# Other places in TensorE's queue for the ends of the mixer's branches and for x's transposes, in a two-layer hybrid encoder

## The chip, the cores and the metric

The kernel runs on one core of a Trainium2 chip. The metric is the device time of one execution in microseconds (us); the time before is the median of three runs. Names used throughout: PE is TensorE (matmuls and transposes), ACT is ScalarE, DVE is VectorE, POOL is GpSimd, SP is SyncE, which starts the weight loads. PSUM is the memory that matmuls write to. Every engine works through its own queue in order; an instruction at the head of a queue that waits for another engine holds up all that stands behind it.

## The reference

The input x is 256 tokens by 1024 features, float32; there are two layers. In each:

```python
xn = rms_norm(x, norm_mix_g[l]);  h = xn @ w_in[l]      # all branches and 4 merge gates from one product
ya = conv_module(glu, ...)        # GLU, depthwise conv of width 31, LayerNorm over channels, silu
yb = gla_branch(gq, gk, gv, gr, glr, ...)   # chunked gated linear attention, then RMS over each head, * silu(gr)
yc = window_attention(q, k, v, sink)        # softmax(q k) v, 4 heads
yd = pool_branch(pin, ...)                  # mean pooling of widths 2 to 16, minus self, per-group map
proj   = einsum('btnc,ncd->btnd', stack([ya, yb, yc, yd]), w_branch)   # each branch, 256 -> 1024
merged = sum(sigmoid(gate) * proj, axis=2)
x = x + merged @ w_out
x = x + square(relu(rms_norm(x, norm_ffn_g) @ w_up)) @ w_down           # 1024 -> 4096 -> 1024
```

and a final RMSNorm.

## The kernel before

**Matrix products.** Each float32 product is done as three matmuls on operands split into a high and a low part: hi·hi, lo·hi and hi·lo. In mm3 (L303 to L305) the weights are stationary and 256 tokens stream; in mm3t (L312 to L314) the activations are stationary and 512 columns of weights stream. So L303, L304, L305 and L312, L313, L314 are nearly all of PE's work, and a row's "mm<-hi,ysh" says whose: xh/xl are the normalised x of the mixer, ysh/ysl the split output of a branch, mh/ml the merged branches, fh/fl the input of the MLP, hh/hl its hidden values.

**Weights** come in pieces of 128 x 1024 values. SP loads a piece into a raw buffer, ACT casts it to hi (L276), DVE subtracts to get lo (L277). The pieces form one list in order of use and are split four ahead of PE. Raw has three buffers, hi and lo five each.

**Order.** The code is written as a program order with priorities; a scheduler turns it into one queue for each engine. Work inside `urgent()` gets a priority 4000 higher, so that it goes ahead of what was written earlier and is ready at the same time. `tc.issue_after(ins)` puts work behind the instruction `ins` on its engine. PSUM tiles come from two pools of four buffers: mm (mmt) for the large products, ax (axt) for the rest, the transposes among them.

**A layer's mixer.** After the input products, attention and GLA are generators; the string TURNS hands out six turns to attention and twelve to GLA. Then `conv_branch` writes the whole convolution branch. The gates and the branches' projections follow in the order of GATE_SEQ: gate A (pooling), gate B (attention) and so on, each in two halves of 512 columns, with the projection ("br") of a branch some steps behind its gate:

```python
GATE_SEQ = (("gate", A, 0), ("gate", A, 1),
    ("gate", B, 0), ("br", A, 0), ("gate", B, 1), ("br", A, 1),
    ("gate", C, 0), ("br", B, 0), ("gate", C, 1), ("br", B, 1),
    ("gate", L, 0), ("br", C, 0), ("gate", L, 1),
    ("br", L, 0), ("br", C, 1), ("br", L, 1))     # B attention, C GLA, L convolution
```

A gate is 48 matmuls, a projection 12. The scheduler mixes the branches' small instructions into the gates' matmuls. The ends of the branches are these chains:

- Attention: transposes of its result (L654 on PE), then split_y: ACT casts to ysh (L447), DVE subtracts to ysl (L448).
- GLA: the product with the state (L853 on PE), squares (L864 and L865 on ACT), the load of ACT's table for Ln and Exp (L866), sums over a head (L871 and L872 on PE), a reciprocal square root (L332 and L333 on ACT, then L335 to L337 on DVE), a product (L876 on DVE), split_y.
- Convolution: taps on DVE and ACT; a sum over channels for the mean (L524 on PE), L525 on DVE, a square on ACT (L527) with a table load (L528) behind it, the sum for the variance (L532 on PE), the reciprocal square root, a Tanh with its table load (L540), split_y.

**Around the MLP.** The out projection accumulates in ax; DVE adds it to x in two halves of 512 columns (L1087). turn_x then transposes x back (L431 on PE, 128 x 128 blocks, eight a half), and split_x makes fh (L420, ACT) and fl (L421, DVE) of it. The same turn_x makes xh and xl for the next layer, after DVE has added the MLP's result to x (L1150).

Of the kernel before, what the change touches and what calls it, by code (L numbers as in the profile page):

```python
# [171 lines left out]
def trunk_kernel(ctx: ExitStack, tc: tile.TileContext, x, w, prm, wup, poolw, cst, out, depth, dbg=None):  # L172
# [125 lines left out]
    def mm3(o, wt, k, c0, xs, kx, start, stop):  # L298
        wh, wl = wt
        xh, xl = xs  # L300
        a = wh[:, k, c0 : c0 + P]
        b = wl[:, k, c0 : c0 + P]
        mm(o, a, xh[:, kx, :], start=start, stop=False, skip_group_check=True)  # L303
        mm(o, a, xl[:, kx, :], start=False, stop=False, skip_group_check=True)  # L304
        mm(o, b, xh[:, kx, :], start=False, stop=stop, skip_group_check=True)  # L305

# [187 lines left out]

    def conv_branch(l):
# [48 lines left out]

# [4 lines left out]
    def attention_branch(l, qkv, y):  # L549
# [76 lines left out]
        for it in range(2):  # L626
            for jt in range(2):
                tp = axt((P, 4, P))
                for h in range(4):
                    nc.tensor.transpose(tp[:, h, :], ps_[it][:, h % 2, h // 2, jt * P : (jt + 1) * P], ident)  # L630
                S.copy(pt[:, jt, :, it * P : (it + 1) * P], tp)

            ot = axt((P, 4, 64))
            for h in range(4):
                g = h // 2
                for jt in range(2):
                    mm(  # L637
                        ot[:, h, :],
                        pt[:, jt, h, it * P : (it + 1) * P],
                        qkv[:, jt, 384 + 64 * g : 448 + 64 * g],  # L640
                        start=jt == 0,
                        stop=jt == 1,
                    )
            V.tensor_tensor(
                on[:, it].rearrange("p (g r) e -> p g r e", g=2),
                ot.rearrange("p (g r) e -> p g r e", g=2),
                dens[it].rearrange("p r g -> p g r").unsqueeze(3).broadcast_to([P, 2, 2, 64]),
                ALU.mult,
            )
            yield  # L650
        o = axt()
        for it in range(2):
            for g in range(2):
                nc.tensor.transpose(  # L654
                    o[:, g, it * P : (it + 1) * P], on[:, it, 2 * g : 2 * g + 2].rearrange("p h e -> p (h e)"), ident
                )
        y[BR_ATT] = split_y(o)

# [17 lines left out]

    def gla_gates(l, glr, wup_t):
        gt = axt((P, 2, P))
# [11 lines left out]
        z = axt()  # L690
        for d in range(2):
            mm(z[:, d, :], wur[:, d, :], glt, start=True, stop=True)
        zb = g2()
# [16 lines left out]
    def gla_branch(l, px, qk, v, gy, ys):  # L710
# [150 lines left out]
        with urgent():  # L861
# [5 lines left out]
            V.tensor_tensor(sl, sq, sh.bitcast(F32), ALU.subtract)  # L867
            V.tensor_tensor(gy, gy, o, ALU.mult)
            ss = axt()
            for t in range(2):  # L870
# [23 lines left out]
    for l in range(depth):  # L894
# [32 lines left out]
        def gvl(i, k0, k1):  # L927
            wt = piece(l, ("gvl", i))
            for k in range(k1 - k0):
                for it in range(2):  # L930
                    mm3t(gps[it], xs, k0 + k, it, wt, k, k0 + k == 0, k0 + k == 7)

        def part256(ps, key, i):
            wt = piece(l, (key, i))
            for k in range(4):
                for t in range(2):
                    kk = 4 * i + k
                    mm3(ps[:, t, :], wt, k, t * P, xs, kk, kk == 0 and t == 0, kk == 7)

        cuts = list(enumerate(GVL_CUTS[l == 0]))  # L940
        for i, (k0, k1) in cuts if l == 0 else cuts[:2]:
            gvl(i, k0, k1)
        ps_g, ps_a = mmt(), None
# [13 lines left out]
        for it in range(2):  # L957
            gla_in(l, gps[it], it, v, glr, R)
        px = gla_gates(l, glr, wup_t)

        for i in range(2) if l == 0 else (1,):
# [3 lines left out]
        for i in range(2) if l == 0 else (1,):  # L965
            part256(ps_a, "glu0", i)
        conv_in(ps_a, ps_g, R)
# [42 lines left out]

        def gate(n, h):
            pss = [mmt((P, 512)) for _ in range(2)]
            for i in range(4):
                wt = piece(l, (("gate", n, h), i))
                for k in range(2):
                    for it in range(2):
                        kk = 2 * i + k
                        mm3t(pss[it], xs, kk, it, wt, k, kk == 0, kk == 7)
            for it in range(2):
# [22 lines left out]
        def turn_merged(h):  # L1042
            for f in (2 * h, 2 * h + 1):
                with urgent():
# [36 lines left out]
        for h in range(2):  # L1081
            for i in (2, 3):
                out_part(i, h)
# [16 lines left out]
        def up(c, parts=(0, 1)):  # L1100
# [3 lines left out]
            for i in parts:  # L1104
                wt = piece(l, (("up", c), i))
                for k in range(4):
                    for t in range(2):
                        kk = 4 * i + k
                        mm3(ps[:, t, :], wt, k, t * P, fx, kk, kk == 0 and t == 0, kk == 7)
            if 1 not in parts:  # L1110
                return
            r = gh_p.tile([P, 2, T], F32, tag="gh", name=nm("r"))
# [21 lines left out]
        for i in range(2):  # L1134
            for c in range(2):
                up(c, (i,))
        with urgent():
# [14 lines left out]
        if nxt < depth:  # L1152
            xh = xs_p.tile([P, KD, T], F32R, tag="xs", name=nm("xh"))
            xl = xs_p.tile([P, KD, T], F32R, tag="xs", name=nm("xl"))
            for h in range(2):
                for c in (14, 15):
                    down(c, (0, 1), (h,))
                for it in range(2):
                    add_mlp(it, h)
                turn_x(xh, xl, h, col(nxt, 0, 8))  # L1160
                for it in range(2):
# [134 lines left out]
```

## Time and profile before

| what | value |
|---|---|
| time, median of 3 runs | 818.33 us (817.81 to 819.58) |
| the profiled execution, its whole time | 819.2 us |
| its span, first to last instruction | 817.4 us |
| PE busy in the span | 783.1 us (96%) |
| ACT busy | 468.5 us (57%) |
| DVE busy | 559.2 us (68%) |
| mean granted TensorE clock | 0.990 of full speed |

The profile shows one execution. An engine's busy time excludes its waits; the granted clock is the share of full speed (2.4 GHz) at which TensorE was allowed to run, 0.50 being 1.2 GHz. A matmul's duration in a row is longer than its step, since matmuls overlap: at full clock L312 to L314 start 0.23 us apart and each lasts 0.39 us. In a row, "[1.23 <-ACT g L864]" is the idle time ahead of the instruction, and the instruction that ended it.

### The profile page before, as it was taken

To read this page: it belongs to the slowest core of one execution; us is meant where nothing else is said; L and a number is where in the kernel's file an instruction comes from. 1 tells how busy PE (TensorE), PEld (TensorE's weight loads), DVE (VectorE), ACT (ScalarE), POOL (GpSimd) and SP (SyncE) were. 2 spreads that over 40 slices of the span, in tenths; PEclk is the share of its full clock that TensorE was granted. 3 is DMA by queue.
4 is the path that set the end of the run, shared out by engine and by line. 5 is a ranking of instruction groups with operands and counts; after the bars stand their busy time and mean duration, and the time that the engine had idled before them with its cause. 6 is when DMAs were issued, how large, how long until landed. Compare 5 with 4: busy or idle time off the path is not lost.

```text
span 817.4 us, 12270 instructions
## 1 busy us (share of the span) xinstructions
PE 783.1 (96%) x4782; PEld 687.4 (84%) x4782; DVE 559.2 (68%) x801; ACT 468.5 (57%) x704; POOL 7.3 (1%) x20
## 2 busy tenths in 40 slices
PE   6999998799999999999999999959999999999996
PEld 6898887587898999999899988848878999999995
DVE  6789998767665555555577999966586555555553
ACT  6688795454564454444468788664545444444443
POOL 2000000000000000000000000000000000000000
PEclk9999999799999999999999999989999999999999
DMA  8755544165546555555555664515654565566531
GB/s 266 229 182 169 169 133 149 35 203 186 174 162 193 186 185 186 196 181 185 156 177 177 183 186 130 169 64 154 187 178 151 174 211 183 188 188 190 184 126 52
DMA packets 40986, 138.55 MB, mean 170 GB/s; under 512 B 4384, under 2 KB 7136, under 8 KB 40928
## 3 DMA queue, kind: packets, MB, share of 16 engines
q1 hardware_dynamic: 39728, 137.15, 53.3%
q8 instruction: 37, 0.61, 0.3%
q10 hardware_dynamic: 1200, 0.62, 0.3%
q14 instruction: 21, 0.17, 0.1%
HBM read 136.71 MB, written 1.05 MB: 169 GB/s over the span
## 4 chain that ended last, share of the span: by engine, by line
PE 89%; DVE 4%; ACT 3%; DMA 3%; issue 1%; SPq 0%; ACTq 0%; DVEq 0%
PE mm L312 10%; PE mm L313 10%; PE mm L314 10%; PE mm L304 9%; PE mm L305 9%; PE mm L303 9%; PE ax L312 9%; PE ax L313 9%; PE ax L314 9%; DMA raw<-in_w_dram 2%; DVE lo L277 1%; ACT hi L276 1%; PE ax L637 1%; PE ax L814 1%; DMA xT<-in_x_dram 1%
## 5 line engine op out<-in xcount | busy, mean ns | idle before, releaser
L277 DVE TENSOR_TENSOR lo<-raw,hi 128x1024 fp32r<-128x1024 f32 (+2 forms) x260 | 314.1, 1209 | 211.6 <-ACT hi L276 210.8
L276 ACT CAST hi<-raw 128x1024 fp32r<-128x1024 f32 (+2 forms) x260 | 269.4, 1037 | 288.3 <-PE mm L304 101.2
L304 PE MATMUL mm<-fl,hi 128*128 128x256 f32 x512 | 145.1, 284 | 0.7 <-DVE fl L421 0.7
L303 PE MATMUL mm<-fh,hi 128*128 128x256 f32 x512 | 144.4, 283 | 0.7 <-ACT fh L420 0.7
L305 PE MATMUL mm<-fh,lo 128*128 128x256 f32 x512 | 144.7, 283 | 0.0
L312 PE MATMUL mm<-hi,xh 128*128 128x512 f32 (+1 forms) x320 | 124.6, 393 | 6.2 <-ACT hi L276 6.2
L313 PE MATMUL mm<-lo,xh 128*128 128x512 f32 (+1 forms) x320 | 124.8, 390 | 0.0
L314 PE MATMUL mm<-hi,xl 128*128 128x512 f32 (+1 forms) x320 | 122.5, 387 | 0.0
L304 PEld LDWEIGHTS mm<-fl,hi 128*128 128x128 f32 x512 | 98.1, 192 | 2.7 <-DVE fl L421 1.6
L313 PE MATMUL ax<-lo,hh 128*128 128x512 f32 x256 | 100.0, 391 | 0.0
L312 PE MATMUL ax<-hi,hh 128*128 128x512 f32 x256 | 100.0, 391 | 0.0
L303 PEld LDWEIGHTS mm<-fh,hi 128*128 128x128 f32 x512 | 97.8, 192 | 2.2 <-ACT fh L420 1.1
L305 PEld LDWEIGHTS mm<-fh,lo 128*128 128x128 f32 x512 | 98.1, 192 | 0.2
L314 PE MATMUL ax<-hi,hl 128*128 128x512 f32 x256 | 97.7, 389 | 0.0
L312 PEld LDWEIGHTS mm<-hi,xh 128*128 128x128 f32 x320 | 61.6, 194 | 18.3 <-ACT hi L276 6.6
L313 PEld LDWEIGHTS mm<-lo,xh 128*128 128x128 f32 x320 | 61.9, 194 | 12.3 <-DVE lo L277 0.6
L314 PEld LDWEIGHTS mm<-hi,xl 128*128 128x128 f32 x320 | 61.6, 193 | 11.6 <-issue 0.2
L314 PEld LDWEIGHTS ax<-hi,hl 128*128 128x128 f32 x256 | 47.9, 188 | 10.0
L312 PEld LDWEIGHTS ax<-hi,hh 128*128 128x128 f32 x256 | 48.2, 188 | 9.3
L313 PEld LDWEIGHTS ax<-lo,hh 128*128 128x128 f32 x256 | 48.2, 188 | 8.9
L305 PE MATMUL mm<-xh,lo 128*128 128x256 f32 x160 | 45.3, 284 | 0.0
L304 PE MATMUL mm<-xl,hi 128*128 128x256 f32 x160 | 45.2, 283 | 0.0
(261 smaller groups left out, 1005.2 us busy)
## 6 DMA issues: line engine op xcount, KB each, us to landing
raw<-in_w_dram SPq DMA_DIRECT2D x252, 512.0 KB, 3.7
raw<-in_w_dram SPq DMA_DIRECT2D x6, 288.0 KB, 2.9
xT<-in_x_dram SPq DMA_DIRECT2D x4, 256.0 KB, 5.1
cst_t<-in_cst_dram SPq DMA_DIRECT2D x1, 608.0 KB, 8.0
out_dram<-yo SPq DMA_DIRECT2D x2, 256.0 KB, 2.4
out_dram<-yo ACTq DMA_DIRECT2D x2, 256.0 KB, 2.3
raw<-in_w_dram SPq DMA_DIRECT2D x1, 432.0 KB, 6.4
poolw_t<-in_poolw_dram SPq DMA_DIRECT2D x2, 128.0 KB, 4.8
```

What stands on the lines that cost most here:

```text
L276: S.copy(h[:, :n], r[:, :n])
L277: V.tensor_tensor(lo[:, :n], r[:, :n], h[:, :n].bitcast(F32), ALU.subtract)
L303: mm(o, a, xh[:, kx, :], start=start, stop=False, skip_group_check=True)
L304: mm(o, a, xl[:, kx, :], start=False, stop=False, skip_group_check=True)
L305: mm(o, b, xh[:, kx, :], start=False, stop=stop, skip_group_check=True)
L312: mm(o, xh[:, kx, tk], wh[:, k, :], start=start, stop=False)
L313: mm(o, xh[:, kx, tk], wl[:, k, :], start=False, stop=False)
L314: return mm(o, xl[:, kx, tk], wh[:, k, :], start=False, stop=stop)
L637: mm(ot[:, h, :], pt[:, jt, h, it * P : (it + 1) * P], qkv[:, jt, 384 + 64 * g : 448 + 64 * g], start=jt == 0, stop=jt == 1,)
L814: mm(ps[32 * b : 32 * b + 32, jt], kk[:, j0 : j0 + 32], q[:, :, j0 : j0 + 32], start=True, stop=True, tile_position=(0, 32 * b),)
```

## The change

- `conv_branch` becomes a generator with two yields. Its first part (taps and the first sum on DVE) stays where the branch was written. The mean (L524 before, L530 after) is put behind the last matmul of the first projection of attention, ("br", B, 0). The variance and all that follows (L532 before, L540 after) is put behind the second piece of the gate ("gate", C, 1).
- GLA gets one more yield, ahead of its sums over a head (L871 and L872 before, L884 and L885 after). A call behind ("br", B, 0) would continue it. The generator now has nine yields and needs ten turns; TURNS hands it twelve, so its end is still written inside the loop over TURNS.
- The last parts of attention, the second product and the transposes with split_y, become urgent.
- `turn_x` is put behind a given matmul. For the MLP, half 0 stands behind the out projection's piece 2 of half 1 and half 1 behind the first piece of the MLP's first product; for the next layer, half 0 stands behind the down projection's chunk 14 of half 1 and half 1 behind the first piece of that layer's gvl product.
- The products of GLA's forget gates (z) are put behind the glu0 product.

```diff
-    def turn_x(xh, xl, h, g):
-
+    def turn_x(xh, xl, h, g, behind):
+
+        with tc.issue_after(behind.ins):
+            turn_x_now(xh, xl, h, g)
...
@@ conv_branch
             s = br.tile([P, T], F32, tag="cv_s", name=nm("cs"))
             V.tensor_tensor(s, acc[:, 0, :], acc[:, 1, :], ALU.add)
+        yield
+        with urgent():
             mu = axt((P, 512))
             mm(mu[:, :T], onesd, s, start=True, stop=True)
...
             V.tensor_tensor(s, sq[:, 0, :], sq[:, 1, :], ALU.add)
+        yield
+        with urgent():
             var = axt((P, 512))
             mm(var[:, :T], onesd, s, start=True, stop=True)
...
-            return split_y(y)
+            ys[BR_CONV] = split_y(y)
...
@@ attention_branch
+        with urgent():
+            o = axt()
+            for it in range(2):
+                for g in range(2):
+                    nc.tensor.transpose(
+                        o[:, g, it * P : (it + 1) * P], on[:, it, 2 * g : 2 * g + 2].rearrange("p h e -> p (h e)"), ident
                     )
...
-        y[BR_ATT] = split_y(o)
+            y[BR_ATT] = split_y(o)
...
@@ gla_branch
             V.tensor_tensor(gy, gy, o, ALU.mult)
+        yield
+        with urgent():
             ss = axt()
...
-        assert len(y) == 3
-        y[BR_CONV] = conv_branch(l)
+        conv = conv_branch(l, y)
+        next(conv)
...
+                if i in steps:
+                    with tc.issue_after(done.ins):
+                        next(steps[i], None)
...
+        ENDS = {("gate", C, 1): ({1: conv},)}
         for what, n, h in GATE_SEQ:
-            done = (gate if what == "gate" else project)(n, h)
+            done = (gate if what == "gate" else project)(n, h, *ENDS.get((what, n, h), ()))
+            if (what, n, h) == ("br", B, 0):
+                with tc.issue_after(done.ins):
+                    next(conv)
+                    next(turns["g"], None)
...
-            turn_x(fh, fl, h, col(l, 8, 8))
...
+                if (i, h) == (2, 1):
+                    turn_x(fh, fl, 0, col(l, 8, 8), done)
...
-                up(c, (i,))
+                done = up(c, (i,))
+                if (i, c) == (0, 0):
+                    turn_x(fh, fl, 1, col(l, 8, 8), done)
```

The change moves PE's queue at the end of layer 0's mixer, from GLA's product with the state on; before (L853 state, L871/L872 GLA's sums, L654 attention's transposes, L524/L532 convolution's sums, L312 with ysh the projection of attention):

```order
L853 MATMUL ax_1072<-St_789,v_272 64x128 x8
L871 MATMUL ax_1093<-g_191_1086,o64r 128x256
L654 MATMUL ax_1111<-cst_t,t_138_819 128x128
L524 MATMUL ax_1215<-cs_1213,onesd 128x256
L654 MATMUL ax_1111<-cst_t,t_138_819 128x128 x3
L872 MATMUL ax_1093<-g_192_1087,o64r 128x256
L871 MATMUL ax_1093<-g_191_1086,o64r 128x256
L872 MATMUL ax_1093<-g_192_1087,o64r 128x256
L532 MATMUL ax_1223<-cs_1221,onesd 128x256
L312 MATMUL mm_1687<-hi_1607,ysh_1116 128x512
L313 MATMUL mm_1687<-lo_1608,ysh_1116 128x512
```

And after (L864 state, L884/L885 GLA's sums, L664 transposes):

```order
L864 MATMUL ax_1072<-St_789,v_272 64x128 x8
L664 MATMUL ax_1093<-cst_t,t_138_819 128x128 x2
L884 MATMUL ax_1102<-g_191_1086,o64r 128x256
L885 MATMUL ax_1102<-g_192_1087,o64r 128x256
L884 MATMUL ax_1102<-g_191_1086,o64r 128x256
L885 MATMUL ax_1102<-g_192_1087,o64r 128x256
L312 MATMUL mm_1658<-hi_1578,ysh_1098 128x512
L313 MATMUL mm_1658<-lo_1579,ysh_1098 128x512
```

Attention's transposes now stand ahead of GLA's sums, and convolution's two sums are gone from this place: they stand 30 and 73 rows behind the first L312 with ysh, among the matmuls of the gates.

ACT's queue over the same stretch, before (ysh from t or g is a branch's split, the one from ax attention's):

```order
L866 ACT_TABLE_LOAD
L332 ACTIVATE g_194_1098<-ax_1093,epsd 128x512
L527 ACTIVATE t_220_1218<-cacc_1124 128x512
L528 ACT_TABLE_LOAD
L333 ACTIVATE g_194_1098<-g_194_1098 128x512
L332 ACTIVATE crs_1225<-ax_1223,epsd 128x256
L333 ACTIVATE crs_1225<-crs_1225 128x256
L688 CAST g_753_4185<-wup_t_4011 96x256
L447 CAST ysh_1107<-g_196_1105 128x512
L447 CAST ysh_1116<-ax_1111 128x512
```

And after:

```order
L877 ACT_TABLE_LOAD
L451 CAST ysh_1098<-ax_1093 128x512
L332 ACTIVATE g_197_1107<-ax_1102,epsd 128x512
L333 ACTIVATE g_197_1107<-g_197_1107 128x512
L698 CAST g_759_4245<-wup_t_3993 96x256
L276 CAST hi_1688<-raw_1612 128x1024
L451 CAST ysh_1116<-g_199_1114 128x512
```

Attention's cast to ysh now follows the first table load at once, where eight instructions stood between them. In the whole program ACT has 19 table loads, where it had 15.

In layer 1 the projection of attention stands ahead of GLA's product with the state. PE's queue there, after:

```order
L664 MATMUL ax_4909<-cst_t,t_831_4635 128x128 x2
L853 MATMUL ax_4888<-g_825_4612,spad 128x128 x2
L664 MATMUL ax_4909<-cst_t,t_831_4635 128x128 x2
L312 MATMUL mm_5474<-hi_5394,ysh_4914 128x512
L313 MATMUL mm_5474<-lo_5395,ysh_4914 128x512
```

There L853 is a product ahead of the one with the state, which comes 22 rows after the first L312 here. At the start of layer 0's MLP, PE's queue had the second half's transposes (the ninth L431 and the seven behind L303) ahead of the first L304:

```order
L431 MATMUL ax_2264<-cst_t,xt 128x128
L303 MATMUL mm_2287<-fh_2073,hi_2168 128x256
L303 MATMUL mm_2318<-fh_2073,hi_2186 128x256
L431 MATMUL ax_2273<-cst_t,xt 128x128
L431 MATMUL ax_2264<-cst_t,xt 128x128
...
L304 MATMUL mm_2287<-fl_2074,hi_2168 128x256
```

After, from the last transpose of the first half on:

```order
L431 MATMUL ax_2235<-cst_t,xt 128x128
L303 MATMUL mm_2269<-fh_2073,hi_2168 128x256
L303 MATMUL mm_2318<-fh_2073,hi_2186 128x256
L304 MATMUL mm_2269<-fl_2074,hi_2168 128x256
L305 MATMUL mm_2269<-fh_2073,lo_2169 128x256
```

All eight transposes of the second half now stand behind 39 of the MLP's matmuls; the first half's eight stand where they stood.

## Rows read from the trace of the kernel before

**Rows 1.** The page: the span, then busy time of each engine.

```profile
span 817.4 us, 12270 instructions
...
PE 783.1 (96%) x4782; PEld 687.4 (84%) x4782; DVE 559.2 (68%) x801; ACT 468.5 (57%) x704; POOL 7.3 (1%) x20
```

**Rows 2.** TensorE's waits: line, what it waited for, total us, times, longest us.

```profile
PE mm L312 <- ACT ysh L447: 10.4, 2, 5.2
...
PE ax L532 <- DVE cs L530: 3.7, 2, 1.8
PE ax L871 <- ACT g L864: 2.4, 2, 1.2
...
PE ax L431 <- DVE xt L1150: 1.0, 1, 1.0
```

**Rows 3.** TensorE's timeline, layer 0: start, us, line, operation, count, idle time before.

```profile
137.62 1.14 PE L853 MATMUL ax<-St,v 128*64 128x128 f32 x16
139.99 0.36 PE L871 MATMUL ax<-g,o64r 128*128 128x256 f32 x1 [1.23 <-ACT g L864]
...
140.29 0.59 PE L524 MATMUL ax<-cs,onesd 128*128 128x256 f32 x2
140.73 0.49 PE L654 MATMUL ax<-cst_t,t 128*128 128x128 f32 x3
...
143.72 0.67 PE L532 MATMUL ax<-cs,onesd 128*128 128x256 f32 x2 [1.85 <-DVE cs L530]
149.57 0.79 PE L312 MATMUL mm<-hi,ysh 128*128 128x512 f32 x1 [5.18 <-ACT ysh L447]
...
168.90 0.39 PE L312 MATMUL mm<-hi,xh 128*128 128x512 f32 x1
```

**Rows 4.** ScalarE's timeline in the same stretch.

```profile
139.25 0.60 ACT L864 ACTIVATE g<-ax 128x512 fp32r<-128x512 f32 x1
...
140.35 1.28 ACT L866 ACT_TABLE_LOAD   x1
...
143.14 1.28 ACT L528 ACT_TABLE_LOAD   x1
144.43 0.63 ACT L333 ACTIVATE g<-g 128x512 f32<-128x512 f32 x1
...
148.94 0.58 ACT L447 CAST ysh<-ax 128x512 fp32r<-128x512 f32 x1
```

**Rows 5.** Stretches: us, busy time (count) of each engine, granted TensorE clock, DMA.

```profile
149.50:155.00 5.50, 5.43 (x13) 4.26 (x14) 3.63 (x7) 2.55 (x4) 0.23 (x1) 0.50 0.00 0
155.00:156.00 1.00, 1.00 (x5) 0.76 (x4) 0.00 (x0) 0.00 (x0) 0.00 (x0) 0.63 0.00 0
547.70:551.00 3.30, 3.28 (x8) 2.60 (x9) 2.43 (x5) 2.52 (x3) 0.00 (x0) 0.50 0.02 5
551.00:553.00 2.00, 2.00 (x9) 1.59 (x8) 0.69 (x1) 0.00 (x0) 0.00 (x0) 0.83 0.00 0
806.00:809.00 3.00, 1.37 (x11) 1.01 (x10) 1.94 (x8) 2.16 (x10) 0.00 (x0) 1.00 0.00 0
```

**Rows 6.** TensorE's timeline, layer 1, the same place.

```profile
535.76 1.14 PE L853 MATMUL ax<-St,v 128*64 128x128 f32 x16
...
547.72 0.79 PE L312 MATMUL mm<-hi,ysh 128*128 128x512 f32 x1 [5.18 <-ACT ysh L447]
...
566.04 0.39 PE L312 MATMUL mm<-hi,xh 128*128 128x512 f32 x1
```

**Rows 7.** TensorE's timeline at the start of layer 0's MLP.

```profile
226.01 1.36 PE L431 MATMUL ax<-cst_t,xt 128*128 128x128 f32 x9
...
228.07 0.93 PE L431 MATMUL ax<-cst_t,xt 128*128 128x128 f32 x7
229.16 0.38 PE L304 MATMUL mm<-fl,hi 128*128 128x256 f32 x1 [0.17 <-DVE fl L421]
```

**Rows 8.** TensorE's timeline at the start of layer 1.

```profile
411.18 0.98 PE L431 MATMUL ax<-cst_t,xt 128*128 128x128 f32 x7 [0.97 <-DVE xt L1150]
```

More of the change, by code (lines that the diff above doesn't have):

```diff
@@ L304, in mm3 @@
         mm(o, a, xl[:, kx, :], start=False, stop=False, skip_group_check=True)
-        mm(o, b, xh[:, kx, :], start=False, stop=stop, skip_group_check=True)
+        return mm(o, b, xh[:, kx, :], start=False, stop=stop, skip_group_check=True)
     def mm3t(o, xs, kx, it, wt, k, start, stop):
@@ L432, in turn, with turn_x_now @@
         return ps
-    def turn_x(xh, xl, h, g):
+    def turn_x(xh, xl, h, g, behind):
+        with tc.issue_after(behind.ins):
+            turn_x_now(xh, xl, h, g)
+    def turn_x_now(xh, xl, h, g):
         for f in (2 * h, 2 * h + 1):
@@ L493, in trunk_kernel, with conv_branch @@
     n_tap = [0]
-    def conv_branch(l):
+    def conv_branch(l, ys):
         wc = br.tile([P, 62], F32, tag="cv_w", name=nm("wc"))
@@ L626, in attention_branch @@
         for it in range(2):
-            for jt in range(2):
-                tp = axt((P, 4, P))
-                for h in range(4):
[L630 to L642, printed above, removed]
-                    )
@@ L644, in attention_branch @@
[L644 to L656, printed above, removed]
@@ L657, in attention_branch @@
-        y[BR_ATT] = split_y(o)
+            with urgent():
+                for jt in range(2):
+                    tp = axt((P, 4, P))
+                    for h in range(4):
+                        nc.tensor.transpose(tp[:, h, :], ps_[it][:, h % 2, h // 2, jt * P : (jt + 1) * P], ident)
+                    S.copy(pt[:, jt, :, it * P : (it + 1) * P], tp)
+                ot = axt((P, 4, 64))
+                for h in range(4):
+                    g = h // 2
+                    for jt in range(2):
+                        mm(
+                            ot[:, h, :],
+                            pt[:, jt, h, it * P : (it + 1) * P],
+                            qkv[:, jt, 384 + 64 * g : 448 + 64 * g],
+                            start=jt == 0,
+                            stop=jt == 1,
+                        )
+                V.tensor_tensor(
+                    on[:, it].rearrange("p (g r) e -> p g r e", g=2),
+                    ot.rearrange("p (g r) e -> p g r e", g=2),
+                    dens[it].rearrange("p r g -> p g r").unsqueeze(3).broadcast_to([P, 2, 2, 64]),
+                    ALU.mult,
+                )
@@ L675, in gla_qk, with gla_gates @@
             S.copy(qpad[r, h, :], qk[r, 0, :])
-    def gla_gates(l, glr, wup_t):
+    def gla_gates(l, glr, wup_t, behind):
         gt = axt((P, 2, P))
@@ L690, in gla_gates @@
         z = axt()
-        for d in range(2):
-            mm(z[:, d, :], wur[:, d, :], glt, start=True, stop=True)
+        with tc.issue_after(behind.ins):
+            for d in range(2):
+                mm(z[:, d, :], wur[:, d, :], glt, start=True, stop=True)
         zb = g2()
@@ L868, in gla_branch @@
             V.tensor_tensor(gy, gy, o, ALU.mult)
+        yield
+        with urgent():
             ss = axt()
@@ L930, in gvl @@
                 for it in range(2):
-                    mm3t(gps[it], xs, k0 + k, it, wt, k, k0 + k == 0, k0 + k == 7)
+                    done = mm3t(gps[it], xs, k0 + k, it, wt, k, k0 + k == 0, k0 + k == 7)
+            return done
         def part256(ps, key, i):
@@ L937, in part256 @@
                     kk = 4 * i + k
-                    mm3(ps[:, t, :], wt, k, t * P, xs, kk, kk == 0 and t == 0, kk == 7)
+                    done = mm3(ps[:, t, :], wt, k, t * P, xs, kk, kk == 0 and t == 0, kk == 7)
+            return done
         cuts = list(enumerate(GVL_CUTS[l == 0]))
         for i, (k0, k1) in cuts if l == 0 else cuts[:2]:
-            gvl(i, k0, k1)
+            done = gvl(i, k0, k1)
+            if l and i == 0:
+                turn_x(xh, xl, 1, col(l, 0, 8), done)
         ps_g, ps_a = mmt(), None
@@ L958, in trunk_kernel @@
             gla_in(l, gps[it], it, v, glr, R)
-        px = gla_gates(l, glr, wup_t)
         for i in range(2) if l == 0 else (1,):
@@ L965, in trunk_kernel @@
         for i in range(2) if l == 0 else (1,):
-            part256(ps_a, "glu0", i)
+            done = part256(ps_a, "glu0", i)
+        px = gla_gates(l, glr, wup_t, done)
         conv_in(ps_a, ps_g, R)
@@ L1009, in trunk_kernel, with gate @@
         last_cast = []
-        def gate(n, h):
+        def gate(n, h, steps={}):
             pss = [mmt((P, 512)) for _ in range(2)]
@@ L1017, in gate @@
                         kk = 2 * i + k
-                        mm3t(pss[it], xs, kk, it, wt, k, kk == 0, kk == 7)
+                        done = mm3t(pss[it], xs, kk, it, wt, k, kk == 0, kk == 7)
+                if i in steps:
+                    with tc.issue_after(done.ins):
+                        next(steps[i], None)
             for it in range(2):
@@ L1082, in trunk_kernel @@
             for i in (2, 3):
-                out_part(i, h)
+                done = out_part(i, h)
+                if (i, h) == (2, 1):
+                    turn_x(fh, fl, 0, col(l, 8, 8), done)
             for it in range(2):
@@ L1108, in up @@
                         kk = 4 * i + k
-                        mm3(ps[:, t, :], wt, k, t * P, fx, kk, kk == 0 and t == 0, kk == 7)
+                        done = mm3(ps[:, t, :], wt, k, t * P, fx, kk, kk == 0 and t == 0, kk == 7)
             if 1 not in parts:
-                return
+                return done
             r = gh_p.tile([P, 2, T], F32, tag="gh", name=nm("r"))
@@ L1156, in trunk_kernel @@
                 for c in (14, 15):
-                    down(c, (0, 1), (h,))
+                    done = down(c, (0, 1), (h,))
+                    if (c, h) == (14, 1):
+                        turn_x(xh, xl, 0, col(nxt, 0, 8), done)
                 for it in range(2):
                     add_mlp(it, h)
-                turn_x(xh, xl, h, col(nxt, 0, 8))
                 for it in range(2):
```

## The prediction

> **What bounds the kernel now.** I read the page first: PE is busy for 783.1 of a span of 817.4 us and no other engine comes near it [rows 1]. So the time is PE's work plus PE's idle time, 34.3 us, plus what a low clock adds. The profiled execution took 819.2 us, 1.8 more than its span and 0.9 more than the median of 818.33. The sum below starts from 819.2; the prediction takes 0.9 off again.
>
> Then the list of PE's waits [rows 2]. The largest that a change of order can touch are four: the projection of attention waits for its ysh 5.2 us in each layer, convolution's variance sum 1.8 to 1.9, GLA's first sum 1.2, and at the start of layer 1 a transpose waits 1.0 for x. PE's timeline shows that the first three lie end to end [rows 3]: from 138.76 (L853's start plus its 1.14) to 149.57 PE has only a dozen small records. ACT's timeline says why the third is long [rows 4]. Attention's transposes ended near 141.2 (140.73 + 0.49), but its cast to ysh started at 148.94, because ACT's queue holds ahead of it GLA's reciprocal root, convolution's square, a second table load and GLA's own split. Attention is ready and waits for two branches that are needed later.
>
> The last view is the table of stretches [rows 5]. After this stop the granted clock is 0.50 from 149.5 to 155 and 0.63 for one more us, in layer 1 0.50 from 547.7 to 551 and 0.83 for two more: the lower level, 1.2 GHz. PE was busy nearly all of it, so the loss is 5.43 x 0.5 + 1.0 x 0.37 = 3.1 us in layer 0 and 3.28 x 0.5 + 2.0 x 0.17 = 2.0 in layer 1.
>
> **Part 1: layer 0's mixer, −9.5.** After the change the queues hold: L853 (now L864), two transposes of attention, GLA's four sums, then the projection with ysh. ACT goes from the first table load straight to attention's ysh. GLA's part ahead of that load is unchanged, so the load again ends at 140.35 + 1.28 = 141.63 [rows 4]; the transposes are done by then. The cast takes 0.58 to 0.62 and the projection starts at 142.25 in place of 149.57. From there to the first matmul of gate L PE needed 168.90 − 149.57 = 19.33 us, of which 3.1 was the low clock: 16.2 at full clock. Convolution's two sums must now be done among these matmuls. L524's record is 0.59, L532's 0.67, but the next row starts 0.44 behind L524 [rows 3]; I take 0.45 each, 0.9 together (1.3 by the records). So gate L starts at 142.25 + 16.2 + 0.9 = 159.4, where it was 168.90: −9.5. What remains idle is 138.76 to 142.25 less GLA's four sums, some 2.5 us.
>
> Does the clock fall in that rest? From 806 to 809 PE was busy for 1.37 of 3.0 us and kept 1.00 [rows 5]; here it is busy about 0.9 of 3.5. That is the nearest row, a little busier than this case; I take no fall, and keep a fall of 1 to 3 us for the range (2.0 and 3.1 were the prices of the long stops). The Trainium skill, "TensorE: Matmul & The Clock Gate", Part 1, says that activity releases the throttle and idling brings it back. Rows 5 agree in direction: the clock is low behind the stops of 5.18 us. By that rule alone the rest could bring a fall too, which would make the sum about 3 us worse.
>
> **Part 2: layer 1's mixer, −9.6.** Here the projection of attention goes ahead of the product with the state as well. PE reached that product at 535.76 [rows 6]. Ahead of it are now attention's four transposes (0.27 + 0.49 in layer 0's place, 0.5 on the engine), and DVE's last product for them and the cast each come late, for which I allow 1.0 together from the instructions queued ahead of them. The projection starts at 535.76 + 0.5 + 1.0, about 537.2. To gate L it was 566.04 − 547.72 = 18.32, less 2.0 for the clock: 16.3. Into it go the product with the state (1.14), GLA's sums (0.9) and convolution's (0.9), which lay ahead of it or in the stop before. Gate L starts at 537.2 + 16.3 + 2.9 = 556.4, where it was 566.04: −9.6. GLA's chain now runs under gate matmuls, so its 1.2 wait goes too.
>
> **What hides the moved chains.** ACT's Ln and Tanh now alternate with the gates' Tanh, so four more table loads, 1.28 each [rows 4], two a layer. Behind the load at 143.14 the next instruction starts at 144.43, so I charge nothing on top. ACT is busy 468 of 817 us [rows 1] and the gates give it slack; by my count the Tanh that frees gate L's PSUM ends at 157.7 in layer 0 (PE comes at 159.4), and at 556.3 in layer 1, where PE comes at 556.4. That cover is thin. If it is gone, each further us of ACT's chain is a us of PE. The Trainium skill, "ScalarE: Activation LUTs", What ACT_TABLE_LOAD costs, puts 1.38 us of drain on each 1.28 us load. That speaks against this change. The trace does not agree, since the two rows at 143.14 and 144.43 leave 0.01 between load and next start; by the page the two loads would cost layer 1 some 2.8 us and layer 0 nothing to 1.1.
>
> **Part 3: the MLP's start, +1.0 in each layer.** The first half's transposes stay behind the last matmul of the out projection; only the second half's move. Before, PE filled the time in which DVE made fl with seven transposes of the second half (0.93) and waited only 0.17 for it [rows 7]. After, fl comes no sooner: DVE's x, lo and fl are the same chain. So L304 still starts at 229.16, PE idles about 1.1, and the transposes come 39 matmuls later at full price: +0.93. Behind them the second half's split queues with the casts of weights on ACT and DVE, a wait of up to 0.8; the small waits of before there (0.2 and less) go. I take +1.0 a layer, +2.0 in all, with bounds of +0.5 and +2.0 a layer.
>
> **Part 4: layer 1's start, +0.5.** The transpose that waited 0.97 for x at 411.18 belongs to the second half [rows 8]. It goes behind the first piece of gvl; its wait is covered. But the first product still waits for xh and xl, whose chain on ACT and DVE ends only some 0.7 sooner, and the 0.95 of transposes is paid later. Net +0.5 by my count, between −1.0 (the whole wait is won) and +1.0.
>
> The forget gates' z and the urgent middle of attention move work under the input products and gates, which have other matmuls at hand; I charge 0 (bounds −0.5 and +1).
>
> **Sum.** 819.2 − 9.5 − 9.6 + 2.0 + 0.5 = 802.6 for an execution like the profiled one; less 0.9 for the median, 801.7. I say 802.
>
> **Rivals.**
> - *A new stop takes part of the gain.* In-order queues have to carry convolution's chain between the gates: its variance on ACT stands behind gates' Tanhs and ahead of casts, layer 1's margin is 0.1, and the rest in layer 0 may bring the low clock. Price: 2 to 4 us for a wait in one or both layers, or 3.1 for the clock in layer 0. Time 804.5 to 809. For it: the thin margins. Against: a gate gives PE 48 matmuls 0.23 us apart, 11 us, while such a chain runs.
> - *The change does less than it says: attention's ysh still comes late.* GLA's last call is idle and its end is still written inside TURNS, so in layer 0 GLA's sums stand ahead of the projection. If GLA's sums came out later than L872 did (141.26), ysh itself would not wait, but PE would. If the projection waits as far as the end of GLA's Ln and Exp, about 3 us a layer are left of the stop and the clock falls again: 801.7 + 2 x 3 + 5 = 813. ACT's order speaks against it.
> - *More is won.* Part 4 wins its wait and part 3 costs only 0.5 a layer: 801.7 − 1.5 − 1.0 = 799.
> - *Slower than before.* Casts of weights stand in ACT's queue behind convolution's square and Ln, which wait for PE, whose next piece needs those casts. Each such circle stops PE until the chain comes through. It decides only if it takes over 17 us: the stop of before (1.23 + 1.85 + 5.18, and 3.1 of clock, 11.4) would have to come back at new places in both layers on top of parts 3 and 4: 801.7 + 2 x 11.4 = 824.5. Against it: the pieces are split four ahead, and each is 12 matmuls, 2.7 us of PE, in a gate.
>
> **Chances.** The forecast with its own range of 799.5 to 804.5: 0.62. More won (under 799.5): 0.08. A new stop (804.5 to 809): 0.20. Ysh still late (809 to 816): 0.06. Slower or no change: 0.04. The range 798.5 to 809.5 leaves out 0.06 + 0.04 above and some 0.05 below, with the bounds of parts 3 and 4 inside. A measurement of this kernel can tell about 0.2%, 1.6 us, from no change. Faster by more: 0.95, within: 0.02, slower: 0.03.
>
> **What would show it.** PE's row of the first matmul with ysh at 142 to 143 and 537 to 538, with the wait ahead of it under 1.5; granted clock 1.00 in the 10 us behind; the first matmuls of gate L near 159.4 and 556.4 on the span's clock; no wait over 0.5 for cs, crs or a gate's Tanh. At the MLP's start a wait of about 1.1 ahead of the first L304, once in each layer, which is new. The prediction is wrong if the list of PE's waits holds a line of over 2 us that is not there now, or if the clock's row shows 0.50 after 142.

## The result

The changed kernel took 805.76 us (median of 4, 805.58 to 807.65), the kernel before 818.78 in the same comparison: a ratio of 0.9847, interval 0.9828 to 0.9866. That is 13.0 us faster; 802 was forecast, with a range of 798.5 to 809.5. The page of the profiled execution, which is the 807.65 one (first the span, then each engine's busy time):

```profile
span 805.8 us, 12281 instructions
...
PE 782.1 (97%) x4782; PEld 687.2 (85%) x4782; DVE 558.3 (69%) x801; ACT 473.9 (59%) x708; POOL 8.0 (1%) x20
```

PE's idle time fell from 34.3 to 23.7 us. From the list of PE's waits after:

```profile
PE mm L304 <- DVE fl L421: 2.9, 4, 0.9
...
PE mm L312 <- ACT xh L420: 1.2, 1, 1.2
...
PE ax L885 <- DVE g L878: 0.9, 1, 0.9
...
PE ax L884 <- ACT g L875: 0.9, 1, 0.9
PE mm L312 <- ACT ysh L451: 0.7, 1, 0.7
```

Against [rows 2], the 10.4 us for ysh have become 0.7, convolution's 3.7 are gone, and GLA's 2.4 are 1.8. At layer 1's start a product now waits 1.2 for xh, where a transpose waited 1.0 for x. Much longer than before is the wait in the first line shown, at the MLP's start for fl. In the list of the kernel before it reads:

```profile
PE mm L304 <- DVE fl L421: 0.7, 4, 0.2
```

PE's timeline at the end of layer 0's mixer, to be laid beside [rows 3]:

```profile
138.56 1.14 PE L864 MATMUL ax<-St,v 128*64 128x128 f32 x16
139.64 0.44 PE L664 MATMUL ax<-cst_t,t 128*128 128x128 f32 x2
140.94 0.35 PE L884 MATMUL ax<-g,o64r 128*128 128x256 f32 x1 [0.86 <-ACT g L875]
...
142.21 0.50 PE L885 MATMUL ax<-g,o64r 128*128 128x256 f32 x1 [0.92 <-DVE g L878]
...
143.23 0.79 PE L312 MATMUL mm<-hi,ysh 128*128 128x512 f32 x1
```

and ACT's, of which the last two rows lie later, between the gates:

```profile
141.29 1.28 ACT L877 ACT_TABLE_LOAD   x1
142.59 0.58 ACT L451 CAST ysh<-ax 128x512 fp32r<-128x512 f32 x1
...
154.95 1.28 ACT L534 ACT_TABLE_LOAD   x1
156.25 1.05 ACT L276 CAST hi<-raw 128x1024 fp32r<-128x1024 f32 x1
```

PE comes to the state product 0.94 later than before (138.56 against 137.62), and all that follows is the forecast's chain, shifted by this: the projection at 143.23 where 142.25 + 0.94 = 143.19 was due. But its first row lasts 0.79, the duration that [rows 3] show at the low clock. The table of stretches, of which some overlap (us, busy time of PE, PEld, DVE, ACT and POOL, granted clock, DMA):

```profile
138.50:142.00 3.50, 1.93 (x20) 1.29 (x19) 1.68 (x2) 3.48 (x6) 0.00 (x0) 1.00 0.06 22
139.70:143.23 3.53, 1.66 (x8) 0.96 (x7) 2.45 (x4) 3.50 (x6) 0.00 (x0) 0.87 0.15 41
142.00:144.00 2.00, 1.70 (x5) 1.31 (x6) 1.44 (x3) 1.96 (x4) 0.00 (x0) 0.58 0.64 213
142.50:143.00 0.50, 0.50 (x3) 0.34 (x2) 0.25 (x1) 0.49 (x2) 0.00 (x0) 0.50 0.66 147
144.00:146.00 2.00, 2.00 (x7) 1.57 (x6) 1.39 (x2) 0.52 (x1) 0.00 (x0) 0.57 0.13 49
612.00:614.00 2.00, 1.85 (x13) 1.85 (x14) 1.56 (x7) 1.00 (x4) 0.00 (x0) 0.84 0.61 160
614.00:616.00 2.00, 2.00 (x11) 2.00 (x11) 0.00 (x0) 0.00 (x0) 0.00 (x0) 0.50 0.39 156
616.00:618.00 2.00, 2.00 (x16) 2.00 (x15) 0.00 (x0) 0.00 (x0) 0.00 (x0) 0.81 0.00 0
```

The clock fell to 1.2 GHz (0.50) at the end of the rest that was left in layer 0, the stretch before the projection in which PE has little to do, and again at the start of layer 1's MLP. Busy time times the missing share gives 1.70 x 0.42 + 2.0 x 0.43 = 1.6 us and 1.85 x 0.16 + 1.0 + 0.38 = 1.7 us. PE's timeline there, beside [rows 7] (layer 0's start shows the same waits without the fall):

```profile
609.00 1.03 PE L431 MATMUL ax<-cst_t,xt 128*128 128x128 f32 x8
610.72 0.50 PE L303 MATMUL mm<-fh,hi 128*128 128x256 f32 x2 [0.68 <-ACT fh L420]
612.15 0.39 PE L304 MATMUL mm<-fl,hi 128*128 128x256 f32 x1 [0.93 <-DVE fl L421]
...
618.17 1.04 PE L431 MATMUL ax<-cst_t,xt 128*128 128x128 f32 x8
...
621.04 0.39 PE L304 MATMUL mm<-fl,hi 128*128 128x256 f32 x1 [0.53 <-DVE fl L421]
```

The second half's transposes no longer fill the wait, cost their own time later, and bring a second wait of 0.53. In layer 1 the projection of attention starts here:

```profile
532.45 0.50 PE L312 MATMUL mm<-hi,ysh 128*128 128x512 f32 x1 [0.68 <-ACT ysh L451]
```

### The profile page after: what moved, and what is told of

It is laid out like the page before. It is cut to its first block, busy times and chain, and to the rows that moved or that the text cites. A ratio compares the mean times of both kernels' runs of the same rounds, so it can differ in the third digit from the quotient of the medians.

```text
span 805.8 us, 12281 instructions
## 1 busy us (share of the span) xinstructions
PE 782.1 (97%) x4782; PEld 687.2 (85%) x4782; DVE 558.3 (69%) x801; ACT 473.9 (59%) x708; POOL 8.0 (1%) x20
## 4 chain that ended last, share of the span: by engine, by line
PE 91%; DVE 4%; ACT 2%; DMA 2%; issue 1%; SPq 0%; ACTq 0%; DVEq 0%
PE mm L312 10%; PE mm L313 10%; PE mm L314 10%; PE mm L304 10%; PE mm L305 9%; PE mm L303 9%; PE ax L312 9%; PE ax L313 9%; PE ax L314 9%; DVE lo L277 2%; DMA raw<-in_w_dram 1%; ACT hi L276 1%; PE ax L646 1%; PE ax L825 1%; DMA xT<-in_x_dram 1%
## 5 line engine op out<-in xcount | busy, mean ns | idle before, releaser
L304 PE MATMUL mm<-fl,hi 128*128 128x256 f32 x512 | 145.3, 285 | 2.9 <-DVE fl L421 2.9
L303 PE MATMUL mm<-fh,hi 128*128 128x256 f32 x512 | 144.4, 285 | 1.4 <-ACT fh L420 1.4
L312 PE MATMUL mm<-hi,xh 128*128 128x512 f32 (+1 forms) x320 | 124.2, 392 | 7.7 <-ACT hi L276 6.5
L304 PEld LDWEIGHTS mm<-fl,hi 128*128 128x128 f32 x512 | 98.7, 193 | 4.8 <-DVE fl L421 3.7
L303 PEld LDWEIGHTS mm<-fh,hi 128*128 128x128 f32 x512 | 98.3, 193 | 2.9 <-ACT fh L420 1.8
L312 PE MATMUL ax<-hi,hh 128*128 128x512 f32 x256 | 100.0, 390 | 0.0
L312 PEld LDWEIGHTS mm<-hi,xh 128*128 128x128 f32 x320 | 60.9, 192 | 20.5 <-ACT hi L276 7.0
L312 PEld LDWEIGHTS ax<-hi,hh 128*128 128x128 f32 x256 | 48.2, 188 | 9.2
L304 PE MATMUL mm<-xl,hi 128*128 128x256 f32 x160 | 45.2, 283 | 0.0
```

Source lines behind the costliest of these rows:

```text
L312: mm(o, xh[:, kx, tk], wh[:, k, :], start=start, stop=False)
```

## The experiments

Twelve kernels ran, in three sets; in each set the kernel before was timed beside them (medians 818.67, 818.54 and 818.32). These lie within 0.5 us of each other and of the 818.78 above, so medians of different sets are compared as they stand. Where traces are compared, it is one execution of each kernel. The first set takes parts away from the change, or starts from before.

**x's transposes as before**, the rest as changed:

```diff
-                if (i, h) == (2, 1):
-                    turn_x(fh, fl, 0, col(l, 8, 8), done)
...
+            turn_x_now(fh, fl, h, col(l, 8, 8))
...
-                if (i, c) == (0, 0):
-                    turn_x(fh, fl, 1, col(l, 8, 8), done)
...
-            if l and i == 0:
-                turn_x(xh, xl, 1, col(l, 0, 8), done)
```

> The changed kernel with x's transposes where they were before, around the MLP and at the next layer's start; everything else as changed. Theory (parts 3 and 4, mis-sized): the trace after shows 0.94 of wait ahead of the first L304 and 0.53 for the second half's fl, in both layers, and in layer 1 the granted clock falls behind it. Undone, 1.45 a layer and 0.4 at layer 1's start come back: 805.8 - 3.3 = 802.5, and 801 where the clock's fall goes too. Rival (the shortfall of 4 us lies in the mixers alone, and the transposes cost the 2.5 of the prediction or less): 803.3 to 805.8.

Measured: 803.04 us, ratio 0.9810 (0.9795 to 0.9825), 2.7 below the change: between the two, near the prediction's own 2.5. Its trace has the MLP's start of [rows 7] again and no fall of the clock there, but still one behind layer 0's mixer.

**Attention's end not urgent**, the rest as changed (two `with urgent():` taken away in attention_branch):

> The changed kernel with attention's end not urgent; everything else as changed. Theory A (urgency is what brings ysh forward): without it the stop of layer 0's mixer returns, 810 to 818. Theory B (what brought it forward is that convolution and GLA's sums moved away, and urgency only changed the scheduler's order): in this kernel's queues the cast to ysh stands ahead of GLA's squares and table load, and the projection ahead of GLA's sums, so the projection of layer 0 starts about 2.4 us sooner than in the change (143.23), pays 0.9 for the sums later and keeps the clock at 1.00: 802.5 to 804.5.

Measured: 803.16, ratio 0.9811 (0.9798 to 0.9825). Theory B holds in this: urgency was not what brought ysh forward, and it costs 2.6 us. The projection starts at 140.20, and the clock stays at 1.00 behind the mixers; it fell at the start of layer 0's MLP instead (0.50 from 220 to 222). Theory B's other half, that moving convolution away had a share, does not survive the runs below.

**Convolution at one place**, ahead of the gates, the rest as changed:

```diff
         conv = conv_branch(l, y)
-        next(conv)
+        for _ in conv:
+            pass
...
-                    next(conv)
```

> The changed kernel with convolution's branch written at one place, ahead of the gates, as before; attention's end urgent and everything else as changed. Theory (the projection waited for attention's ysh behind the other branches in ACT's queue, so urgency alone brings most of the gain, and convolution's sums cost only where PE waits for them): here one of its sums stands ahead of the projection, but none that waits long; 804 to 807. Rival (convolution's chain of sums was the stop): 812 to 818.

Measured: 805.31, ratio 0.9838 (0.9820 to 0.9856), not to be told from the change. Convolution's set places were not needed for the gain. Its trace has no fall of the clock behind layer 0's mixer, but one at the start of layer 0's MLP (0.59 from 220 to 222).

**Attention urgent and GLA's yield alone**, on the kernel before:

> The kernel before with one part of the change alone: attention's end urgent, and GLA's end a step later in the generator. Convolution, x's transposes and the forget gates' z as before. Theory: the mixers' gain as in the run with convolution undone, without the loss at the MLP and the layer's start (3.3) and the 0.3 for z: 800.5 to 803.5. Rival (it needs convolution's ends between the gates): 812 to 818.

Measured: 799.66, ratio 0.9776 (0.9760 to 0.9793): 6 us better than the whole change and 0.8 below the theory's span. But this kernel held two edits, and the runs did not yet say which of them does it. The second set parts them. **GLA's yield alone**, on the kernel before:

```diff
             V.tensor_tensor(gy, gy, o, ALU.mult)
+        yield
+        with urgent():
             ss = axt()
```

> The kernel before with one more yield in GLA ahead of its sums over a head, and nothing else: attention not urgent, convolution at one place, x's transposes and z as before. Theory (the yield alone is what frees the projection: GLA's end is then written behind attention's end, so the scheduler puts attention's cast ahead of GLA's chain): ysh in ACT's queue stands ahead of GLA's squares and of the table load, so layer 0's projection starts near 141; 797.5 to 800.5. Rival (urgency of attention did it): 813 to 819.

Measured: 796.93, ratio 0.9737 (0.9723 to 0.9751), the fastest kernel of the study, 0.6 below the theory's span. PE's timeline of it at the end of layer 0's mixer, then ACT's:

```profile
136.45 0.60 PE L664 MATMUL ax<-cst_t,t 128*128 128x128 f32 x4
136.97 1.15 PE L863 MATMUL ax<-St,v 128*64 128x128 f32 x16
138.81 0.50 PE L312 MATMUL mm<-hi,ysh 128*128 128x512 f32 x1 [0.69 <-ACT ysh L451]
...
143.50 0.28 PE L883 MATMUL ax<-g,o64r 128*128 128x256 f32 x1
```

```profile
138.16 0.59 ACT L451 CAST ysh<-ax 128x512 fp32r<-128x512 f32 x1
138.64 0.61 ACT L874 ACTIVATE g<-ax 128x512 fp32r<-128x512 f32 x1
139.13 0.61 ACT L875 ACTIVATE g<-ax 128x512 f32<-128x512 f32 x1
139.76 1.28 ACT L876 ACT_TABLE_LOAD   x1
```

Attention's cast stands ahead of GLA's squares, and the projection waits 0.69 in place of 5.18. GLA's first sum (L883) comes 4.7 us behind the projection's start, amid matmuls, and its wait of 1.23 is gone. The granted clock stays at 1.00 behind both mixers:

```profile
139.00:142.00 3.00, 3.00 (x14) 2.44 (x14) 2.32 (x4) 2.03 (x3) 0.00 (x0) 1.00 0.46 124
528.00:540.00 12.00, 12.00 (x56) 10.01 (x55) 8.21 (x12) 7.90 (x10) 0.00 (x0) 1.00 0.35 103
```

What is gone adds up to the gain. Of the 10.4 us of waits for ysh 0.7 are left, convolution's 3.7 and GLA's 2.4 are not in the list of PE's waits, and the low clock had cost 3.1 and 2.0: 20.9 of the 21.6 us won.

Why one yield does this can be read from TURNS. GLA's ninth turn, which was its last, is the 14th letter, attention's sixth and last turn the 15th, GLA's tenth the 16th. With the yield GLA's end is written behind attention's end. The same order shows in the queues of the change above: before, GLA's sums have the tile ax_1093 and attention's result ax_1111; after, attention's has ax_1093 and GLA's sums ax_1102. No run shows by which of its rules the scheduler then puts attention first, by the order of writing itself or by the order in which the two get their buffers. Moving attention's last turn ahead of GLA's ninth without the yield was not tried either. **Urgency alone**, on the kernel before:

> The kernel before with attention's end urgent, and nothing else. Theory (the yield did it): ACT's queue still has attention's cast to ysh behind both branches' chains and PE's has all sums ahead of the projection, so the stop of 5.2 us and the low clock behind it stay in both layers; 817 to 819.5. Rival (urgency did it): 799 to 803.

Measured: 819.76, ratio 1.0014 (1.0005 to 1.0023), 0.3 above the theory's span: nothing won, perhaps 1 us lost. Its first waits are those of before:

```profile
PE mm L312 <- ACT ysh L451: 10.4, 2, 5.2
...
PE ax L540 <- DVE cs L536: 3.7, 2, 1.8
PE ax L881 <- ACT g L874: 2.4, 2, 1.2
```

**GLA's yield and convolution's set places**, the rest as before (the diff's edits to conv_branch, gate and ENDS, and the yield):

> The kernel with GLA's yield and convolution's two ends at their set places; attention not urgent, x's transposes and z as before. Against the run with the yield alone it prices convolution's part. Theory (convolution's chain holds nobody up once attention goes first, and its set places cost two more table loads a layer that are hidden): within 1.5 us of the run with the yield alone, 798.5 to 801.5. Rival (the set places are worth a wait of 1.8 us a layer, as L532 had): 3 us below it.

Measured: 797.31, ratio 0.9744 (0.9730 to 0.9758), 0.4 above the yield alone and inside both intervals, as the theory had it; the span it named took the yield alone to be slower than it is. The set places are worth nothing once the projection goes first, and their extra table loads (19 in the program against 17 with the yield alone) cost nothing that these runs can tell.

**Attention urgent, GLA's yield, and attention's last two turns earlier:**

```diff
-TURNS = "agagagagggagggaggg"
+TURNS = "agagagagggagagggggg"
```

> The kernel with attention urgent and GLA's yield, and TURNS with attention's last two turns earlier (agagagagggagagggggg). ACT's queue has attention's cast ahead of GLA's squares and table load in both layers, and PE's the projection ahead of GLA's sums, and the program has 15 table loads again. Theory: the projection of layer 0 waits only for its own cast, about 1.5 us less than with the cast behind the table load; 797 to 799.7. Rival (urgency brings attention's copies ahead of what the gates need, and it costs as much elsewhere): 799.7 to 802.

Measured: 800.11, ratio 0.9774 (0.9760 to 0.9788). The median lies in the rival's span and is not to be told from the 799.66 with the old TURNS, though its interval reaches into the theory's. With the cast ahead of the table load PE came to layer 0's out projection 1.0 us sooner than with the old TURNS (192.78 against 193.82). It then needed 1.5 more from the last product of layer 0's MLP to the first of layer 1's out projection (183.02 against 181.53). So the place of the table load is not all that urgency costs.

The third set prices what was left. **z as before**, the rest as changed (gla_gates ahead of glu1 again, without `issue_after`):

> The changed kernel with the forget gates' z placed as before; everything else as changed. The prediction charged 0 for z. Theory (z is not free: the run with the transposes undone is 3.4 above the one that has urgency and the yield but neither z nor convolution moved, and convolution is worth 0.4): 802.3 to 803.5, with layer 1's projection of attention no longer waiting 0.7 for its cast. Rival (the 3.4 belong to the mix of convolution's ends with urgency): 805 to 806.

Measured: 805.38, ratio 0.9841 (0.9820 to 0.9861). The theory's 802.3 to 803.5 missed, but the median says little: the five executions took 803.32, 804.61, 805.38, 806.03 and 807.18 us at mean clocks of 0.999, 0.997, 0.997, 0.994 and 0.995. The traces say more: from the last product of layer 0's MLP to the first of layer 1's out projection this kernel takes 182.59 us and the change 183.62, so z costs 1.0 there, with the clock at 1.00 in both. **GLA's yield and z's new place**, nothing else:

> The kernel with GLA's yield and the forget gates' z behind glu0, and nothing else of the change. Theory (z alone costs, mostly in layer 1's mixer, where GLA's products with the gates come later): 1.5 to 3.5 above the run with the yield alone (796.9): 798.4 to 800.4. Rival (z costs only beside urgent attention): 796.5 to 797.5.

Measured: 798.56, ratio 0.9756 (0.9742 to 0.9770), 1.6 above the yield alone, with four executions within 0.23 us; the theory holds. In its trace layer 1's projection waits 0.68 for its cast and the state product (1.14) follows it:

```profile
525.85 0.50 PE L312 MATMUL mm<-hi,ysh 128*128 128x512 f32 x1 [0.68 <-ACT ysh L451]
...
531.07 1.14 PE L864 MATMUL ax<-St,v 128*64 128x128 f32 x16
```

With the yield alone the state product filled that wait:

```profile
524.03 1.14 PE L863 MATMUL ax<-St,v 128*64 128x128 f32 x16
525.11 0.50 PE L312 MATMUL mm<-hi,ysh 128*128 128x512 f32 x1
```

**x's transposes as before around the MLP only**, the rest as changed:

> The changed kernel with x's transposes around the MLP as before, and those of the next layer's start at their set places. It splits the 2.7 that the transposes cost together into parts 3 and 4 of the prediction. Theory (trace after: 1.45 a layer at the MLP's start, 0.4 at layer 1's): 2.3 to 2.9 below the change, 802.9 to 803.5. Rival (the layer's start costs half of it): 804 to 805.

Measured: 804.33, ratio 0.9824 (0.9808 to 0.9839), 1.4 below the change. By the median this lies in the rival's span, not in the theory's 2.3 to 2.9; but the two intervals overlap, and its profiled execution had a longer fall of the clock behind layer 0's mixer than the change's (0.80 in the stretch from 140 to 142, 0.50 from there to 148). The traces settle it where the clock is at 1.00. From the last product of layer 0's MLP to the first of layer 1's out projection the change takes 183.62 us, this kernel 183.71 and the one with all transposes as before 183.65: the layer's start costs nothing. From the first product of the out projection to the last of the MLP the change takes 206.42 in layer 0, against 205.31 and 205.33, and 207.94 in layer 1, against 205.30 in both: 1.1, and 2.6 with the 1.7 of the clock's fall. **GLA's yield and attention's last two turns earlier**, not urgent:

> The kernel with GLA's yield, attention not urgent, and attention's last two turns earlier in TURNS (agagagagggagagggggg). The program has 15 table loads and attention's cast ahead of GLA's squares in both layers. Theory (the yield already gives all there is to win at the mixers' ends; earlier turns only reorder): 796.3 to 797.7. Rival (layer 1's last wait of 0.7 for the cast goes and two loads fewer help): 795 to 796.2.

Measured: 798.06, ratio 0.9750 (0.9736 to 0.9764): 1.1 above the yield alone, just outside the theory's span and far from the rival. Fewer table loads and an earlier cast win nothing more.

## Why the prediction was right, and where it was off

The direction and the mechanism at the mixers' ends were right: the stop was attention's cast standing in ACT's queue behind two branches that nobody needed yet. Which part of the change frees it the prediction did not ask, and the runs put it elsewhere than most of the change's moves: in the one yield of GLA. The forecast was 3.8 us too low. The measured time lies above its narrower range of 799.5 to 804.5, in the span of its rival of a new stop, and one of its own signs of being wrong came: the clock's row shows 0.50 after 142. Its other sign, a wait of over 2 us that was not there, came in part: the wait for fl was there with 0.7 and is 2.9 now, but a wait of 1.1 in each layer was forecast. Between the two profiled executions 16.6 were forecast and 11.55 came; of the 5.05 that are missing the two falls of the clock are 3.3. By its steps, from the offsets of PE's rows between the two traces, with the first product of the out projection in each layer before:

```profile
203.29 0.40 PE L312 MATMUL ax<-hi,mh 128*128 128x512 f32 x1
600.46 0.40 PE L312 MATMUL ax<-hi,mh 128*128 128x512 f32 x1
```

and after:

```profile
196.22 0.40 PE L312 MATMUL ax<-hi,mh 128*128 128x512 f32 x1
586.26 0.40 PE L312 MATMUL ax<-hi,mh 128*128 128x512 f32 x1
```

- **Part 1.** From the state product (+0.94) to the out projection (203.29 before, 196.22 after, −7.07) layer 0's stop gave −8.0. With the 1.6 of low clock taken out that is −9.6; −9.5 was forecast. The step that failed is "I take no fall". Its nearest row had PE busy for 1.37 of 3.0 us at a clock of 1.00. In the rest after the change, 139.70 to 143.23, PE was busy for 1.66 of 3.53 us, more than the 0.9 that was forecast, and the clock fell all the same. One row was too little to rule a fall out. The Trainium skill, "TensorE: Matmul & The Clock Gate", Part 1, says that how busy PE has been of late sets the clock; that left a fall open, and the trace agrees in direction: 0.50 at the end of a stretch in which PE was idle for more than half.
- **The forget gates' z and urgent attention, charged 0.** Of the +0.94 ahead of the stop some 0.2 to 0.3 arise at GLA's first transposes, a wait that is 0 to 1.2 in the other kernels' profiles, and the rest among the turns, where the traces without urgency have no such loss. So the 0 was wrong by at most 0.7, within the bound of +1. What the two cost against a kernel without them is more: on the kernel with the yield alone, z costs 1.6 and urgency 2.7 (799.66 against 796.93); taken out of the change, urgency gives back 2.6. Most of that lies inside parts 1 and 2. The forecast followed the new queues as they stand, with the cast behind the table load and GLA's sums ahead of the projection, and did not ask what they would be with each part left out.
- **Part 2 and part 4.** From the end of layer 0's MLP (408.83 to 402.87, −5.96) to layer 1's out projection (600.46 to 586.26, −14.20) the change gave −8.2, where −9.6 + 0.5 was forecast. Part 4 was nothing, by the kernels with x's transposes as before, so part 2 gave −8.2 and had been put 1.4 too large. The projection started at 532.45, which is 538.4 on the clock of before, and not 537.2: the 1.5 allowed ahead of it came out as 2.7. Gate L started at 551.74, which is 557.7 on that clock, where 556.4 was forecast. The thin margin of 0.1 there held: no wait for a gate's Tanh stands in the list.
- **Part 3.** Layer 0's MLP cost 1.1 (−7.07 to −5.96; 1.0 was forecast). Layer 1's cost 2.6 (−14.20 to −11.58), of which 1.7 is the low clock behind its own waits. A fall at this place was not among the rivals.
- **Table loads.** Behind the load at 154.95 the next ACT instruction started at 156.25, 0.02 us after the load's 1.28, as in [rows 4]; the drain of 1.38 us that the Trainium skill, "ScalarE: Activation LUTs", What ACT_TABLE_LOAD costs, adds to a load does not show here either.

The rival "a new stop takes part of the gain" came about in its clock form. The rival "the change does less than it says" named the idle call for GLA rightly, and its time was rightly given little chance; but neither it nor the forecast saw why the idle call does not matter. The yield already has GLA's end written behind attention's end, and it gives 21.6 us by itself. The other parts together give back 8.8: 0.4 (not distinguishable from 0) for convolution, 1.6 for z, 2.7 for urgency and 2.7 for x's transposes make 7.4; the remaining 1.4 is less than the scatter that the falls of the clock bring, and where it comes from is not shown. The kernel with the yield alone, at 796.93, beats both kernels.

## What to carry to other kernels

When a change has several parts, follow the queue of each part alone as well as that of the whole: here one yield, which only changes which of two chains is written first, held more than the whole gain, and each further part cost something or nothing. Urgency alone did not move attention's chain ahead of GLA's, which was as urgent and written earlier; a change in which is written first did, without any urgency for attention. Small work that fills a wait (the transposes here) is free where it stands. Moved, it costs its own time, about 1 us a layer here, since the wait that it had covered stays; and that wait, no longer filled, can bring the clock down too.

## What the runs showed of the hardware

A rest of PE of the same make is followed by a low clock in some executions and not in others. In the changed kernel's trace the start of layer 0's MLP has the waits of layer 1's (0.94 and 0.53 for fl), and the clock fell only in layer 1. With attention not urgent, or convolution at one place, it fell only in layer 0, with z as before in neither. In the profiled executions with the transposes where they were before, it never fell there.

Behind layer 0's mixer the clock fell in the profiled executions of the four kernels with urgent attention and convolution's sums moved away (the change, both kernels with x's transposes put back, and z as before). It stayed at 1.00 with convolution at one place, and with attention urgent and GLA's yield alone, which both leave the sums there: PE was busy for 2.16 and 2.15 us from 138.5 to 142, and for 1.93 in the change. So convolution's set places, worth nothing on the yield alone, may cost a fall of the clock beside urgency; the medians do not show it (805.31 against 805.76).

The same kernel (z as before) ran at mean clocks from 0.994 to 0.999 and took from 803.32 to 807.18 us; the changed kernel ran once at 0.995 (807.65) and three times at 0.997 to 0.998 (805.58 to 805.83). The yield alone, with or without z's new place, stayed at 0.999 to 1.000, and the four executions with z lie within 0.23 us. So a kernel with such rests is not only slower but scatters, here by 1 to 4 us, which is as much as most of the parts under test.
